# Sums of the last two expert groups kept per expert, and down weights loaded as neighbouring rows

## The chip, the cores and the metric

The kernel runs on one core of a Trainium2 chip. The metric is the device time of one execution in microseconds (us). It is compared by the median of several runs. One further execution was recorded by the hardware profiler; its span is counted from the first to the last instruction.

## The reference, cut to what matters

The layer normalises 256 tokens of width 1024, runs two kinds of attention, and adds the result to its input. Then comes a mixture of experts, which is where the change lies. There are 32 experts in four routing groups of eight; every token chooses one routing group and two experts in it.

```python
g = jnp.argmax(g_logits, axis=-1)
top_v, top_e = lax.top_k(e_logits, EXPERTS_PER_TOKEN)          # 2 per token
weight = p_group * jax.nn.softmax(top_v, axis=-1)
...
hid = jax.nn.silu(xc @ w_gate[e]) * (xc @ w_up[e])             # 1024 -> 256
return hid @ w_down[e]                                         # 256 -> 1024
...
y = jnp.zeros((N, D), t.dtype).at[slot_tok].add((out * slot_w[:, None]).astype(t.dtype))
```

Each expert owns three matrices of 1 MB in float32: gate, up and down. The order of the 256 hidden values does not matter, as long as the hidden vector and the rows of the down matrix have the same order.

## The kernel before, in words

**Weights.** Everything that is streamed from HBM is cut into 112 units of 1 MB (the list `units`, lines 77 to 102): 16 for the two projections, then for each expert its gate and up matrix, and its down matrix two experts later. They go into 23 slots of SBUF: a rotating pool `ring` of 16, and seven slots in other pools that become free later. `fill` (line 120) issues the load of the next unit when the unit that had its slot is done; all these loads stand in the queue of SyncE (SP), at line 138, and the very last unit is loaded in three pieces (line 141). A gate or up unit gives each partition 8 neighbouring rows of 1 KB (line 90); a down unit gives partition p the rows p and p + 128 of 4 KB each (line 92).

**One expert.** Each expert has up to 32 token slots. `gate` and `up` (lines 662 and 668) call `half`, 8 matrix products that put four partial sums into the four 32-partition strips of a PSUM bank, and copy the bank into SBUF, gate by ScalarE (ACT, line 665) and up by VectorE (DVE, line 670). `folded` (line 672) transposes these copies on TensorE (PE), four transposes, and DVE adds the partial sums (lines 678 and 680), which gives the hidden values. `down` (line 696) multiplies them with the down unit (line 693); the four column quarters of the result stand in four strips of one bank.

**Groups of four.** Four experts with neighbouring numbers form a group, eight groups in all (these are the kernel's groups, not the routing groups; group 6 is experts 24 to 27, group 7 is 28 to 31). `prep` (line 607) gathers the tokens of the next group: it needs the two 0/1 matrices `Ps` (lines 597 and 599), then 16 matrix products (line 615). For groups 0 to 6, `down` moves the result in four copies to a tile `oG` with 32 partitions for each expert (lines 707 and 709), `weighted` (line 633) multiplies the 0/1 matrix by the routing weights and transposes it once, and `combine` (line 723) adds the whole group to the sums `y` with 8 products of 128 rows (line 728). For group 7, `weighted_last` (line 620) makes four weighted matrices, one for each expert, all in the pass of expert 30, with the one pair of buffers `Ps`; the result of each expert stays in its strips (`moved`, line 711), and `spread` (line 715) adds one expert with 8 products of 32 rows, four strips side by side.

**Order of the work.** PE executes the products in the order in which the program lists them (`pe`, line 647). The main loop (lines 881 to 907) does for expert e: gate of e, fold of e - 1, at the third expert of a group the `combine` of the group before, up of e, at the fourth expert the `prep` of the next group, at the third expert `weighted`, then down of e - 2. The other engines' queues are ordered by the framework as operands become ready. At e = 28 there is `overflow` (line 755): every engine reads a flag and branches past a slow path, which the given data does not enter. After the loop come (lines 908 to 914) the spreads of experts 28 and 29, down of 30, the residual (`residual`, 8 products with the identity), the spread of 30, and `last`: down of 31 in two halves of columns, each followed by its own `moved`, `spread`, copies out of PSUM and two output transfers.

Of the kernel before, what the change touches and what calls it, by code (L numbers as in the profile page):

```python
# [9 lines left out]
F32 = mybir.dt.float32  # L10
# [4 lines left out]
AF = mybir.ActivationFunctionType  # L15
# [36 lines left out]
def hybrid_layer_kernel(ctx: ExitStack, tc: tile.TileContext, x, xt, w_in, w_out, w_gate, w_up, w_down, smalls, relb, out):  # L52
# [33 lines left out]
    def expert_unit(e, i):  # L86
        src = (w_gate, w_up, w_down)[i][e]
        place[e][i] = len(units)
        if i < 2:
            units.append((src.rearrange("(p k) f -> p k f", p=P), KC, 1))  # L90
        else:
            units.append((src.rearrange("(k p) f -> p k f", p=P), 2, 1))

    for e in range(E):
        expert_unit(e, 0)
# [491 lines left out]
    u = 16  # L587
    G = 4
    x2n = x2q.rearrange("t c k p -> t c p k")
    CROSS = [(j, c) for c in range(NC) for j in range(4)]  # L590
    g2p = A_COLS["g2p"][0]

    def places(g, c):
# [23 lines left out]
            gathered(st, q4, pg, 0, P)  # L617
        return st

    def weighted_last(st):  # L620
        t = pools["late"].tile([P, 2048], F32, name="oL", tag="late")
        st["o"], st["pT"] = t[:, :D].rearrange("p (i n) -> p i n", i=G), t[:, D:].rearrange("p (i t) -> p i t", i=G)
        for i in range(G):
            pt = ps.tile([P, 512], F32, name="ptr", tag="tr")
            for c in range(NC):
                q = st["P"][c][1].rearrange("p (j s) -> p j s", j=G)
                e = st["g"] * G + i
                nc.vector.tensor_scalar(q, st["P"][c][0][:, i : i + 1, :].broadcast_to([P, G, CAP]),
                                        W[:, c, e : e + 1], None, op0=ALU.mult)
                pe(nc.tensor.transpose(pt[:, c * P : (c + 1) * P], q.rearrange("p j s -> p (j s)"), ident))  # L630
            nc.scalar.activation(st["pT"][:, i, :], pt[:, :S], AF.Copy)

    def weighted(st):
        g = st["g"]
        if g == E // G - 1:
            return weighted_last(st)
        pt = ps.tile([P, 512], F32, name="ptr", tag="tr")
        for c in range(NC):
            q = st["P"][c][1].rearrange("p (g s) -> p g s", g=G)
            nc.vector.tensor_tensor(q, st["P"][c][0],  # L640
                                    W[:, c, g * G : (g + 1) * G].unsqueeze(2).broadcast_to([P, G, CAP]), op=ALU.mult)
            pe(nc.tensor.transpose(pt[:, c * P : (c + 1) * P], q.rearrange("p g s -> p (g s)"), ident))
        st["pT"] = ex.tile([P, S], F32, name="pT", tag="pT")
        st["o"] = ex.tile([P, D], F32, name="oG", tag="oG")
        nc.scalar.activation(st["pT"], pt[:, :S], AF.Copy)
# [4 lines left out]
    def half(e, st, i, low):  # L650
# [8 lines left out]
                                    start=r == 0, stop=r == KC // ROWS_Q - 1, tile_position=(0, q * CAP)))  # L659
        return t, pg  # L660

    def gate(e, st):
        t, pg = half(e, st, 0, place[e - 1][0] if e else None)
        st["parts"] = t
        nc.scalar.activation(t[:, :HID], pg[:, :HID], AF.Copy)
        return t

    def up(e, st, t):
        _, pg = half(e, st, 1, place[e][0])
        nc.vector.tensor_copy(t[:, HID : 2 * HID], pg[:, :HID])  # L670

    def folded(t):
        pt = ps.tile([P, 512], F32, name="ptr", tag="tr")
# [22 lines left out]
    def down(e, st, hT, low):  # L696
        i = e % G
        dv = unit(place[e][2], low).rearrange("p (c n) -> p c n", c=2)
        pd = ps.tile([P, 512], F32, name="pd", tag="tr")
        down_product(hT, dv, pd, range(2), range(4))  # L700
        if st["g"] == E // G - 1:
            moved(st, i, pd, slice(0, P))
            return
        for j in range(4):
            dst = st["o"][i * CAP : (i + 1) * CAP, j * 256 : (j + 1) * 256]
            if j % 2 == 0:
                nc.scalar.activation(dst, pd[j * 32 : (j + 1) * 32, :256], AF.Copy)  # L707
            else:
                nc.vector.tensor_copy(dst, pd[j * 32 : (j + 1) * 32, :256])  # L709

    def moved(st, i, pd, rows):
        nc.scalar.activation(st["o"][rows, i, :P], pd[rows, :P], AF.Copy)
        nc.vector.tensor_copy(st["o"][rows, i, P:], pd[rows, P:256])  # L713

    def spread(st, i, pairs):
        for j, c in pairs:
            r = slice(j * CAP, (j + 1) * CAP)
            pe(nc.tensor.matmul(y[j][:, c * 256 : c * 256 + 256], st["pT"][r, i, c * P : (c + 1) * P],  # L718
                                st["o"][r, i, :], start=False, stop=i == G - 1 and c == NC - 1, tile_position=(j * CAP, 0)))

    y = []

# [10 lines left out]
            pe(nc.tensor.matmul(y[j][:, c * 256 : c * 256 + 256], ident, res[:, c, j * 256 : (j + 1) * 256],  # L733
                                start=False, stop=False))

    def last(e, st, hT, res):
        dv = unit(place[e][2]).rearrange("p (c n) -> p c n", c=2)
        pd = ps.tile([P, 512], F32, name="pd", tag="tr")
        down_product(hT, dv, pd, (0,), range(4))
        warmed(2, "pp")  # L740
        for nh in range(2):
            down_product(hT, dv, pd, (1,), (2 * nh, 2 * nh + 1))
            moved(st, G - 1, pd, slice(nh * 64, nh * 64 + 64))
            j0 = 2 * nh
            spread(st, G - 1, [(j, c) for c in range(NC) for j in (j0, j0 + 1)])
            for c, eng in enumerate((nc.scalar, nc.sync)):
                for j in (j0, j0 + 1):
                    dst = res[:, c, j * 256 : (j + 1) * 256]
                    if j == j0:
                        nc.scalar.activation(dst, y[j][:, c * 256 : c * 256 + 256], AF.Copy)  # L750
                    else:
                        nc.vector.tensor_copy(dst, y[j][:, c * 256 : c * 256 + 256])  # L752
                eng.dma_start(out[c * P : (c + 1) * P, nh * 512 : nh * 512 + 512], res[:, c, nh * 512 : nh * 512 + 512])

    def overflow():
# [121 lines left out]
    with tc.issue_after(state["ps"].ins):  # L877
        nc.vector.tensor_reduce(cm, pc, axis=AX.X, op=ALU.max)
        nc.vector.tensor_copy(flag, cm)
    before, queue = None, []  # L880
    for e in range(1, E):
        g, i = divmod(e, G)
        old, old_t = st, t
        if i == 0:
            before, st = old, nxt
        t = gate(e, st)
        queue.append((e - 1, old, folded(old_t)))
        if i == 2 and g > 0:
            combine(before)
        up(e, st, t)  # L890
        if i == G - 1 and g < E // G - 1:
            nxt = prep(g + 1)
        if i == 2:
            weighted(st)
        if e == E - 1:
            hT = folded(t)
        if e > 1:
            down(*queue.pop(0), place[e][0])
        if e == OVER_E:
            overflow()  # L900
        if e == E - 1:
            rt_ = ring.tile([P, 2048], F32, name="res", tag="ring")
            res = rt_.rearrange("p (c n) -> p c n", c=NC)
            for c in range(NC):
                for nh in range(2):
                    nc.gpsimd.tensor_copy(res[:, c, nh * 512 : (nh + 1) * 512].rearrange("t (p k) -> t p k", k=KC),
                                          x2n[:, c, nh * 64 : (nh + 1) * 64, :])
    spread(st, 0, CROSS)
    spread(st, 1, CROSS)
    down(*queue.pop(0), place[E - 1][0])  # L910
    residual(0, res)
    residual(1, res)
    spread(st, 2, CROSS)
    last(E - 1, st, hT, res)


_OUTS = [((1, 256, 1024), "float32")]
# [71 lines left out]
```

## Time and profile before

| | |
|---|---|
| median of 3 runs | 344.23 us (343.37 to 344.47) |
| the profiled execution, its own time | 344.96 us |
| its span | 343.2 us |
| PE busy in the span | 314.5 us (92%) |
| DVE, ACT, POOL busy | 194.3, 139.9, 17.3 us |
| mean granted TensorE clock | 0.97 of full speed |
| read from HBM | 121.64 MB |
| SP queue, share of the 16 DMA engines | 89.1% |

The own time is 1.8 us above the span. A matrix product in float32 appears as two PE instructions, so "x16" is 8 products. The duration of a PE row is modelled and rows overlap; the distance between the starts of two rows that follow each other is what the first one costs. "[0.55 <-X]" at the end of a row is idle time of the engine before it and what ended it.

### The profile page before, as it was taken

The page shows a single profiled execution, that of the slowest core. Times are in us where ns is not written, and L with a number is a line of the kernel's source. Part 1 is how long each engine was busy: PE and PEld are TensorE (multiplying, and loading weights), DVE is VectorE, ACT ScalarE, POOL GpSimd, SP SyncE. Part 2 cuts the span into 40 slices and gives each one's busy share as a digit, 9 for nine tenths or more (in the row PEclk, how much of TensorE's full clock was granted, in tenths as well). Part 3 has the DMA queues.
Part 4 walks back from the last instruction along what each step waited for, and adds up shares of the span by engine and source line. Part 5 has one row for each costly group of instructions (what it writes and reads, how often), then busy time and mean ns, then how long its engine had stood idle before and what let it go on. Part 6 is the DMA issues. An engine that isn't in the chain of part 4 may idle for free. (4 is left out here: it accounts for less than half of the span.)

```text
span 343.2 us, 7327 instructions
## 1 busy us (share of the span) xinstructions
PE 314.5 (92%) x2801; PEld 217.4 (63%) x2801; DVE 194.3 (57%) x599; ACT 139.9 (41%) x364; POOL 17.3 (5%) x25
## 2 busy tenths in 40 slices
PE   6999999999999999999999999998489669968893
PEld 2758877788777797576666766566257326625461
DVE  1867858869998658665463654736224522532502
ACT  4876667968886443423232232321112211211302
POOL 1100001000110140000000000000000000040000
PEclk9899999999999999999999999999989978989997
DMA  6999999999635888899999999999999999999903
GB/s 197 403 385 317 389 387 402 413 411 409 209 99 210 319 355 320 303 423 418 416 416 415 415 421 418 413 421 413 416 418 416 418 415 420 416 411 420 362 10 122
DMA packets 29496, 123.20 MB, mean 359 GB/s; under 512 B 2295, under 2 KB 3364, under 8 KB 21268
## 3 DMA queue, kind: packets, MB, share of 16 engines
q1 hardware_dynamic: 28868, 121.17, 89.1%
q0 software_dynamic: 304, 1.02, 1.0%
q8 instruction: 23, 0.38, 0.4%
q10 hardware_dynamic: 288, 0.52, 0.4%
q14 instruction: 13, 0.11, 0.1%
HBM read 121.64 MB, written 1.07 MB: 358 GB/s over the span
## 5 line engine op out<-in xcount | busy, mean ns | idle before, releaser
L658 PE MATMUL pgu<-u,xe 128*32 128x256 f32 x976 | 67.4, 395 | 10.1 <-ACT oG L707 4.8
L254 PE MATMUL pp<-hi,xh 128*128 128x512 f32 (+1 forms) x132 | 53.3, 405 | 2.6 <-ACT hi L243 2.6
L254 PE MATMUL pp<-lo,xh 128*128 128x512 f32 (+1 forms) x132 | 52.1, 399 | 0.3 <-POOL lo L244 0.2
L254 PE MATMUL pp<-hi,xl 128*128 128x512 f32 (+1 forms) x132 | 51.9, 393 | 0.0
L707 ACT ACTIVATE oG<-pd 32x256 f32<-32x256 f32 x56 | 21.0, 374 | 75.0 <-PE pd L693 61.4
L658 PEld LDWEIGHTS pgu<-u,xe 128*32 128x32 f32 x976 | 29.5, 111 | 34.6 <-ACT oG L707 8.6
L244 DVE TENSOR_TENSOR lo<-u,hi 128x512 fp32r<-128x512 f32 x62 | 43.1, 714 | 13.0 <-ACT hi L243 12.7
L243 ACT ACTIVATE hi<-u 128x512 fp32r<-128x512 f32 x64 | 38.9, 626 | 18.3 <-PE pp L254 12.6
L709 DVE COPY oG<-pd 32x256 f32<-32x256 f32 x56 | 23.7, 423 | 38.7 <-ACT oG L707 36.8
L693 PE MATMUL pd<-u,hT 128*32 128x256 f32 x496 | 34.9, 394 | 6.6 <-DMA u<-in_w_down_dram 6.6
L254 PEld LDWEIGHTS pp<-hi,xh 128*128 128x128 f32 x132 | 25.1, 190 | 9.6 <-ACT hi L243 4.0
L254 PEld LDWEIGHTS pp<-lo,xh 128*128 128x128 f32 x132 | 25.3, 192 | 7.4 <-issue 1.0
L254 PEld LDWEIGHTS pp<-hi,xl 128*128 128x128 f32 x132 | 25.2, 191 | 4.6
L670 DVE COPY u<-pgu 128x256 f32<-128x256 f32 x30 | 12.7, 422 | 26.7 <-PE pgu L658 23.6
L615 PEld LDWEIGHTS pg<-Ps,x2q 128*128 128x128 f32 x224 | 25.5, 192 | 2.9 <-DVE gu L678 2.9
L693 PEld LDWEIGHTS pd<-u,hT 128*32 128x32 f32 x496 | 14.5, 112 | 20.0 <-DVE u L670 7.5
L615 PE MATMUL pg<-Ps,x2q 128*128 128x128 f32 x224 | 26.9, 278 | 0.0
L728 PE MATMUL y<-oG,pT 128*128 128x256 f32 x112 | 26.4, 391 | 0.0
L728 PEld LDWEIGHTS y<-oG,pT 128*128 128x128 f32 x112 | 21.8, 200 | 2.8
L678 DVE TENSOR_REDUCE gu<-ptr 128x64 f32<-128x256 f32 x32 | 13.6, 425 | 14.5 <-PE ptr L675 13.8
L675 PEld LDWEIGHTS ptr<-sm,u 128*128 128x128 f32 x120 | 13.4, 147 | 13.1 <-issue 9.9
L675 PE MATMUL ptr<-sm,u 128*128 128x128 f32 x120 | 21.0, 301 | 0.0
(166 smaller groups left out, 342.0 us busy)
## 6 DMA issues: line engine op xcount, KB each, us to landing
u<-in_w_up_dram SPq DMA_DIRECT2D x31, 1024.0 KB, 19.9
u<-in_w_gate_dram SPq DMA_DIRECT2D x30, 1024.0 KB, 19.9
u<-in_w_down_dram SPq DMA_DIRECT2D x30, 1024.0 KB, 19.9
u<-in_w_in_dram SPq DMA_DIRECT2D x11, 1024.0 KB, 12.0
u<-in_w_out_dram SPq DMA_DIRECT2D x4, 1024.0 KB, 14.6
x<-in_w_gate_dram SPq DMA_DIRECT2D x2, 1024.0 KB, 9.0
u<-in_w_in_dram SPq DMA_DIRECT2D x2, 512.0 KB, 6.0
x<-in_x_dram SPq DMA_DIRECT2D x2, 512.0 KB, 10.9
```

What stands on the lines that cost most here:

```text
L243: nc.scalar.activation(hi, raw, AF.Copy)
L244: (nc.gpsimd if u * 4 + k in (0,3,) else nc.vector).tensor_tensor(lo, raw, hi.bitcast(F32), op=ALU.subtract)
L254: yield lambda a=a, w=w, kk=kk, i=i: nc.tensor.matmul(pp, a, w[:, cols], start=first and kk == 0 and i == 0, stop=last and kk == len(hls) ...
L615: pe(nc.tensor.matmul(pg[:, j * P : (j + 1) * P], x2q[:, c, q4 * 4 + j, :], st["P"][c][1], start=c == 0, stop=c == NC - 1))
L658: pe(nc.tensor.matmul(pg[q * CAP : (q + 1) * CAP, :HID], st["xe"][:, k, j0 : j0 + CAP], wv[:, k, :], start=r == 0, stop=r == KC // ROWS_Q ...
L670: nc.vector.tensor_copy(t[:, HID : 2 * HID], pg[:, :HID])
L675: pe(nc.tensor.transpose(pt[:, j * P : (j + 1) * P], t[:, j * P : (j + 1) * P], ident))
L678: nc.vector.tensor_reduce(gu[:, :2], parts[:, :2], axis=AX.X, op=ALU.add)
L693: pe(nc.tensor.matmul(pd[j * 32 : (j + 1) * 32, :256], hT[:, c, :], dv[:, c, j * 256 : (j + 1) * 256], start=c == 0, stop=c == 1, tile_pos ...
L707: nc.scalar.activation(dst, pd[j * 32 : (j + 1) * 32, :256], AF.Copy)
L709: nc.vector.tensor_copy(dst, pd[j * 32 : (j + 1) * 32, :256])
L728: pe(nc.tensor.matmul(y[j][:, c * 256 : c * 256 + 256], st["pT"][:, c * P : (c + 1) * P], st["o"][:, j * 256 : (j + 1) * 256], start=st["g ...
```

## The change

The down unit gives partition p the rows 2p and 2p + 1, which lie side by side in HBM. To give the hidden values the same order, the copies of gate and up read every second element of the PSUM bank, first the even ones, then the odd ones (`paired`). Group 6 is treated like group 7: each expert keeps its own result and weighted matrix, and is added by `spread` one pass after its `down`; the `combine` of group 6 goes. The weighted matrices are made one per pass for group 6 and two per pass at experts 28 and 29 for group 7. Both groups' tiles, and the residual, take a slot of the `ring` pool. The first half of the residual is added in the pass of expert 30. `last` moves, spreads and writes the final expert once, not in two halves.

```diff
-            units.append((src.rearrange("(k p) f -> p k f", p=P), 2, 1))
+            units.append((src.rearrange("(p k) f -> p k f", k=2), 2, 1))
...
+    APART = E // G - 2
...
+    def spare(name):
+        used["ring"].append(len(units))
+        return ring.tile([P, 2048], F32, name=name, tag="ring")
...
+    def repeated(st, i):
+        e = st["g"] * G + i
+        for c in range(NC):
+            q = st["P"][c][1].rearrange("p (j s) -> p j s", j=G)
+            nc.vector.tensor_scalar(q, st["P"][c][0][:, i : i + 1, :].broadcast_to([P, G, CAP]),
+                                    W[:, c, e : e + 1], None, op0=ALU.mult)
+
+    def weighted_last(st, i):
+        pt = ps.tile([P, 512], F32, name="ptr", tag="tr")
+        for c in range(NC):
+            pe(nc.tensor.transpose(pt[:, c * P : (c + 1) * P], st["P"][c][1], ident))
+        nc.scalar.activation(st["pT"][:, i, :], pt[:, :S], AF.Copy)
...
+    def paired(dst, pg):
+        return dst.rearrange("s (c p) -> s c p", c=2), pg[:, :HID].rearrange("s (p c) -> s c p", c=2)
...
-        nc.scalar.activation(t[:, :HID], pg[:, :HID], AF.Copy)
+        nc.scalar.activation(*paired(t[:, :HID], pg), AF.Copy)
...
-        nc.vector.tensor_copy(t[:, HID : 2 * HID], pg[:, :HID])
+        nc.vector.tensor_copy(*paired(t[:, HID : 2 * HID], pg))
...
-        if st["g"] == E // G - 1:
-            moved(st, i, pd, slice(0, P))
+        if st["g"] >= APART:
+            moved(st, i, pd)
             return
...
+    def last(st, hT, dv, pd, res):
         for nh in range(2):
             down_product(hT, dv, pd, (1,), (2 * nh, 2 * nh + 1))
...
+        moved(st, G - 1, pd)
+        spread(st, G - 1)
+        for c in range(NC):
+            for j in range(4):
...
+            for nh, eng in enumerate((nc.scalar, nc.sync)):
                 eng.dma_start(out[c * P : (c + 1) * P, nh * 512 : nh * 512 + 512], res[:, c, nh * 512 : nh * 512 + 512])
...
+            if g >= APART:
+                last_group(st)
         t = gate(e, st)
         queue.append((e - 1, old, folded(old_t)))
-        if i == 2 and g > 0:
+        apart = () if g < APART else (i,) if g == APART else ((0, 1), (2, 3), (), ())[i]
+        if apart:
+            repeated(st, apart[0])
+        if i == 2 and 0 < g <= APART:
             combine(before)
         up(e, st, t)
+        for k, j in enumerate(apart):
+            if k:
+                repeated(st, j)
+            weighted_last(st, j)
         if i == G - 1 and g < E // G - 1:
             nxt = prep(g + 1)
-        if i == 2:
+        if i == 2 and g < APART:
             weighted(st)
+        if done:
+            spread(*done.pop())
...
         if e > 1:
-            down(*queue.pop(0), place[e][0])
+            e2, st2, hT2 = queue.pop(0)
+            down(e2, st2, hT2, place[e][0])
+            if st2["g"] >= APART:
+                done.append((st2, e2 % G))
         if e == OVER_E:
             overflow()
+            res = spare("res").rearrange("p (c n) -> p c n", c=NC)
...
+        if e == E - 2:
+            residual(0, res)
-    spread(st, 0, CROSS)
-    spread(st, 1, CROSS)
+    residual(1, res)
     down(*queue.pop(0), place[E - 1][0])
-    residual(0, res)
-    residual(1, res)
-    spread(st, 2, CROSS)
-    last(E - 1, st, hT, res)
+    spread(*done.pop())
+    dv = unit(place[E - 1][2]).rearrange("p (c n) -> p c n", c=2)
+    pd = ps.tile([P, 512], F32, name="pd", tag="tr")
+    down_product(hT, dv, pd, (0,), range(4))
+    spread(st, 2)
+    warmed(2, "pp")
+    last(st, hT, dv, pd, res)
```

## Rows read from the trace of the kernel before

**Rows 1.** Stretches; after the five engines: granted clock, DMA share, GB/s.

```profile
150.00:200.00 50.00, 50.00 (x633) 33.07 (x635) 27.48 (x79) 14.41 (x41) 0.00 (x0) 1.00 1.02 417
...
250.00:300.00 50.00, 43.67 (x448) 28.03 (x448) 19.41 (x54) 10.04 (x29) 0.00 (x0) 0.90 1.02 417
...
280.00:284.00 4.00, 3.45 (x25) 1.93 (x22) 1.02 (x3) 1.13 (x3) 0.00 (x0) 0.50 1.03 422
...
324.00:328.00 4.00, 4.00 (x66) 2.35 (x64) 1.28 (x4) 0.54 (x2) 0.00 (x0) 1.00 0.39 151
```

**Rows 2.** DMA packets of the span, and issues: count, size, us to landing.

```profile
DMA packets 29496, 123.20 MB, mean 359 GB/s; under 512 B 2295, under 2 KB 3364, under 8 KB 21268
...
u<-in_w_down_dram SPq DMA_DIRECT2D x20, 1024.0 KB, 20.0
```

**Rows 3.** Timeline of SP's queue: start of the issue, its duration, unit.

```profile
209.16 0.33 SPq L138 DMA_DIRECT2D u<-in_w_up_dram  x1
211.63 0.38 SPq L138 DMA_DIRECT2D u<-in_w_down_dram  x1
214.11 0.33 SPq L138 DMA_DIRECT2D u<-in_w_gate_dram  x1
216.68 0.33 SPq L138 DMA_DIRECT2D u<-in_w_up_dram  x1
219.14 0.38 SPq L138 DMA_DIRECT2D u<-in_w_down_dram  x1
221.63 0.33 SPq L138 DMA_DIRECT2D u<-in_w_gate_dram  x1
224.15 0.33 SPq L138 DMA_DIRECT2D u<-in_w_up_dram  x1
```

**Rows 4.** Timeline of PE, experts 26 to 29: start, duration, line, tile.

```profile
280.81 1.94 PE L658 MATMUL pgu<-u,xe 128*32 128x256 f32 x16 [0.55 <-ACT oG L707]
...
292.68 3.84 PE L615 MATMUL pg<-Ps,x2q 128*128 128x128 f32 x32
296.44 1.07 PE L693 MATMUL pd<-u,hT 128*32 128x256 f32 x16
297.33 1.05 PE L658 MATMUL pgu<-u,xe 128*32 128x256 f32 x16
298.31 0.66 PE L675 MATMUL ptr<-sm,u 128*128 128x128 f32 x4
298.90 1.07 PE L658 MATMUL pgu<-u,xe 128*32 128x256 f32 x16
...
304.42 1.07 PE L658 MATMUL pgu<-u,xe 128*32 128x256 f32 x16 [2.46 <-DVEq L758]
```

**Rows 5.** Timeline: `Ps` on DVE, `combine` of group 6, weighted transposes of group 7.

```profile
289.33 0.47 DVE L599 TENSOR_SCALAR Ps<-Pm,rstd 128x128 f32<-128x128 f32 x2
...
312.36 3.62 PE L728 MATMUL y<-oG,pT 128*128 128x256 f32 x16
...
316.91 0.44 PE L630 MATMUL ptr<-sm,Ps 128*128 128x128 f32 x2
...
317.72 0.52 PE L630 MATMUL ptr<-sm,Ps 128*128 128x128 f32 x2 [0.38 <-DVE Ps L628]
```

**Rows 6.** Timeline of the end: spreads, residual, last expert, last copies.

```profile
325.09 2.01 PE L718 MATMUL y<-oL 32*128 32x256 f32 x32
...
328.03 3.72 PE L733 MATMUL y<-res,sm 128*128 128x256 f32 x16
...
331.68 1.15 PE L718 MATMUL y<-oL 32*128 32x256 f32 x16
332.76 0.64 PE L693 MATMUL pd<-u,hT 128*32 128x256 f32 x8
...
335.18 1.13 PE L718 MATMUL y<-oL 32*128 32x256 f32 x8 [0.69 <-DVE oL L713]
...
338.94 0.76 DVE L752 COPY res<-y 128x256 f32<-128x256 f32 x2 [1.26 <-PE y L718]
```

## The prediction before the run

> **What bounds the kernel now.** I read the stretches first, then the queue that issues the weights, then TensorE (PE) in order of time. From 150 us on, the DMA engines are the bound: their share is 1.02 and they move 417 GB/s in the stretches 150 to 200 and 250 to 300 alike [rows 1]. SP's queue says the same in another way: it issues a unit of 1 MB every 2.5 us, and each lands 20 us after its issue [rows 2, 3], so eight are always under way and a new one starts as one ends. In that part PE's time is hidden: it idles 6.3 of the 50 us before 300.
>
> The end looks different. Between 324 and 328 us the rate falls to 151 GB/s, 0.6 MB in four microseconds [rows 1]: the last weights are in by about 327 us. Yet the last copy out of PSUM ends at 338.94 + 0.76 = 339.70 us, and from 325.09 on PE has work almost without a pause: two spreads, down of 30, the residual of 3.72 us, a spread, and then the last expert in two halves, each with its own move, spread and copies [rows 6]. So some 12 us after the weights are a chain of PE, and before it PE had gaps: at the third and fourth expert of a group it runs late because of `combine` (3.62 us) and `prep` (3.84 us), at the other two it waits for weights. Work that leaves the end and goes into those gaps is won. The thing to work out is how much PE can still take between 292 and 327 us.
>
> **The change part by part.** *Down weights.* A down unit consists of 256 packets of 4 KB, a gate or up unit of 128 of 8 KB; the page counts 29496 - 21268 = 8228 packets of 8 KB or more, about the 64 x 128 of gate and up, so rows that lie side by side do travel as one packet [rows 2]. The time of one unit is read from SP's queue: the issue that follows the end of unit n is that of unit n + 8, so the distance from a gate issue to the up issue behind it belongs to a down unit. These distances are 2.57 and 2.52 us, against 2.47, 2.48, 2.46 and 2.49 for the others [rows 3]. I take 0.07 us for each down unit; nothing and 0.10 are the ends. One comes every 7.5 us, so from 150 us to the landing of expert 26's gate at about 281 us there are 17: the weights are 1.2 us earlier there (0 to 1.7), and about 1.5 us earlier at the very end.
>
> *Copies of gate and up with stride two.* No row shows such a read out of PSUM. A copy of 128x256 out of PSUM takes 0.38 us [rows 6]; the ends are nothing and a doubling, 0.4 us more. I take nothing: the fold waits for these copies only a whole gate later (0.98 us [rows 4]); for the last expert a spread of 1.0 us stands between. Without that cover it would be 0.4 us once.
>
> *Slots.* Three tiles now sit in the ring. Worked through `fill`, the last unit then takes the slot of expert 25's gate, not that of 22's down, and that one is free once expert 25 is folded, five experts or some 37 us before the use; a landing takes 20 [rows 2], so the queue of eight is the nearer limit. Cost nothing. SP passes no new instruction before its last load; on POOL the four residual copies only move in the program, since nothing is queued ahead of them and they wait for DVE's branch at `overflow` either way; in the walk below the residual comes 10 us behind that branch.
>
> *PE, walked in program order.* Distances between starts give the prices [rows 4 to 6]: gate 298.31 - 297.33 = 0.98, fold 0.59, up like gate, together 2.55; down 0.89; `prep` 3.76; a spread 2.01 / 2 = 1.0; half the residual 3.65 / 2 = 1.83; the first weighted transpose 0.44, a second behind it 0.81, because DVE must rewrite `Ps` between them [rows 5]. The start is the gate of expert 26, which waited for its weights and then ran at half clock (1.94 us [rows 4], clock 0.50 [rows 1]). PE is late from there to `prep` at 292.68, so this moves with the weights: the up of 27 ends at 292.68 - 1.2 = 291.5.
> Expert 27: transpose 0.44, `prep` 3.76, spread 1.0, down 0.89. A new wait stands here: `Ps` of group 7 can only be written when group 6's last transposes have read it; before, they were written at 289.33, long ahead of `prep` [rows 5]. DVE writes a pair in 0.47 us; I take 0.5, ends 0 and 0.9 (with the copy of up ahead of it in DVE's queue). Behind it waits PE, nobody else. Sum 6.6, so 298.1 (before: 297.33).
> Expert 28: 2.55 + 0.44 + 0.81 + 1.0 + 0.89 = 5.7, so 303.8; then the branch at `overflow`, a hole of 2.46 us [rows 4], so 306.2 (before: 304.42).
> Expert 29: 5.7, so 311.9. Expert 30, without `combine`: 2.55 + 1.0 + 0.89 + 1.83 = 6.3, so 318.2. Expert 31: 2.55 + spread 1.0 + fold 0.59 + down 0.89 + residual 1.83 = 6.9, so 325.0.
> The end: down 0.89, spread 1.0, then first products, warming, second products and move as now (335.18 - 332.76 = 2.42), spread 1.08 between them, the last spread 1.13: 331.6. Four copies on each engine instead of two, 2 x 0.76 + 0.07: 333.1. That is 6.6 us before 339.70. The four output transfers now start within 1 us and not in two pairs 2 us apart; 1 MB at 417 GB/s is 2.5 us, of which about 0.4 cannot hide. **Sum: 6.6 - 0.4 = 6.2 us.** At the first products (326.9) the weights have been there for about 1.4 us, so no more than that could be added if PE were faster. The profiled execution took 344.96 us, so the sum makes 338.8; the median of the runs is 0.7 below it, so the forecast is 344.23 - 6.2 = 338.0.
>
> *A price that the rows dispute.* Each spread uses PE in strips of 32 rows between products of 128 rows, and the change puts seven of these switches into the loop. The spread at 331.68 stands between two such changes and costs 1.08 us, the two at 325.09, which share them, 1.0 each [rows 6]: a change of shape costs less than 0.1 us. The Trainium skill (TensorEngine Tiling (Array Packing), Key Properties) says that changing the tiling mode, not just the tile, drains TensorE. It gives no price; by it the time would be that of the third rival below, which is priced from rows.
>
> **The rivals.** *The packets bring nothing* (the down units stay at the common rate of 417 GB/s, so that the first part of the change does nothing): everything is 1.2 us later, 339.2. For it: the gap of 0.07 rests on six distances. Against: all of them agree.
> *DVE's waits are longer.* At experts 28 and 29 the second `Ps` may queue behind DVE's reductions and the copy of up; with the pair at 1.9 instead of 1.25 twice, 0.4 more at `prep`, and a wait of the same sort, 0.4, at each of experts 24, 25, 30 and 31, the gain shrinks by 3.3: 341.3. Against: at 317.72 the wait was 0.38 us.
> *PE drains.* If PE lets one shape end before the next begins, the overlap of two rows is lost at each switch. A down row lasts 1.07 us and the next one starts 0.89 after it [rows 4], so 0.18 at each of 14 switches, 2.5 us: 340.5. Against: the spread of 1.08 above, whose row of 1.15 still overlaps the next.
> *The clock falls; slower.* If PE, after the hole at `overflow`, runs experts 29 and 30 at half clock, as it ran after its waits before 281 us, each group of 16 instructions costs 0.87 more (1.94 against 1.07 [rows 4]); an expert has gate, up, down, spread and folds, so 3.9 us. It decides from about one and a half experts on; two make 7.8 - 6.2 = 1.6 us slower, 345.8. For it: the hole stays, and the gap at `prep` is new. Against: PE has little idle time between 298 and 318 us in the walk, and the mean clock over 250 to 300 was 0.90 even with the waits of before [rows 1].
>
> **How the numbers follow.** A measurement of this kernel tells about 0.3%, 1.0 us, from no change. Forecast (338.0, own range 336.2 to 339.0) 0.57; no gain from packets 0.13; longer waits 0.13; drain 0.05; clock 0.09; something else 0.03. Low end: the wait at `prep` nothing (0.5), the hole shorter since DVE moves two pieces and not four before its branch (0.8), packets at 0.10 (0.5): 336.2. High end: longer waits and no gain from packets together fall at 342.5; I stop at 342.0, which leaves out the clock, the rest and the worst sums of two, under 0.2. Faster: the first four, 0.88; same: a clock that takes just the 6 us (0.03) and most of the rest (0.02), 0.05; slower: the clock for longer (0.06) and a rest, 0.07.
>
> **What would show it.** In the profile after: `combine` 16 instructions fewer, spreads at each expert from 27 on with 1.0 us between starts; packets of 8 KB up by about 31 x 128; the distances in SP's queue equal; the last copy near 333 and PE's first products of the last expert a little behind its weights; granted clock 1.00 from 288 to 331. Wrong would be: the queue's distances unchanged, a gap before `prep` above 1 us, matmul groups of 1.9 us after 304 us, or spreads that cost clearly more than 1.08 each.

## The result, and the profile after

The changed kernel took 339.76 us (median of 4 runs, 339.21 to 340.34), the kernel before 343.8 beside it: a ratio of 0.9883, interval 0.9859 to 0.9906. That is 4.0 us; the sum had said 6.2. The profiled execution of the changed kernel took 340.34 us with a span of 338.6. The last copy out of PSUM ends 5.7 us earlier than before, the span 4.6 us.

The packets and the queue first, as in [rows 1, 2, 3]: the DMA page with the issue of down units, then SP's queue (start, duration, unit).

```profile
DMA packets 25528, 123.20 MB, mean 364 GB/s; under 512 B 2295, under 2 KB 3364, under 8 KB 13332
...
u<-in_w_down_dram SPq DMA_DIRECT2D x30, 1024.0 KB, 19.8
```

```profile
217.16 0.33 SPq L138 DMA_DIRECT2D u<-in_w_down_dram  x1
219.65 0.33 SPq L138 DMA_DIRECT2D u<-in_w_gate_dram  x1
222.16 0.33 SPq L138 DMA_DIRECT2D u<-in_w_up_dram  x1
```

Packets of 8 KB or more are now 25528 - 13332 = 12196, 3968 = 31 x 128 more, as forecast. The distance from gate to up, the one that belongs to a down unit, is 222.16 - 219.65 = 2.51 here against 2.57 and 2.52 in [rows 3].

Stretches (columns as in [rows 1]: granted clock, DMA share, GB/s at the end):

```profile
250.00:300.00 50.00, 44.70 (x466) 29.28 (x466) 20.11 (x62) 10.30 (x31) 0.00 (x0) 0.93 1.01 420
...
308.00:312.00 4.00, 4.00 (x38) 2.18 (x41) 0.00 (x0) 0.38 (x1) 0.00 (x0) 0.57 1.02 426
324.00:328.00 4.00, 4.00 (x48) 2.44 (x46) 0.69 (x3) 0.38 (x2) 0.00 (x0) 1.00 0.09 32
```

The rate in the bound part went from 417 to 420 GB/s, and between 324 and 328 us there is little left to load (32 instead of 151 GB/s): the weights end earlier. But for four microseconds behind the wait at expert 29 the mean granted clock is 0.57: PE ran most of them at the lower of its two levels.

PE from expert 26 on (start, duration, line, tile, the wait before it), which answers to [rows 4, 6]:

```profile
278.16 1.94 PE L664 MATMUL pgu<-u,xe 128*32 128x256 f32 x16 [1.32 <-DMA u<-in_w_gate_dram]
...
290.27 3.84 PE L615 MATMUL pg<-Ps,x2q 128*128 128x128 f32 x32 [0.37 <-DVE Ps L599]
294.04 1.15 PE L727 MATMUL y<-oL 32*128 32x256 f32 x16
295.11 1.07 PE L702 MATMUL pd<-u,hT 128*32 128x256 f32 x16
296.00 1.05 PE L664 MATMUL pgu<-u,xe 128*32 128x256 f32 x16
...
299.38 0.52 PE L638 MATMUL ptr<-sm,Ps 128*128 128x128 f32 x2 [0.37 <-DVE Ps L632]
...
303.34 1.07 PE L664 MATMUL pgu<-u,xe 128*32 128x256 f32 x16 [1.36 <-DVEq L763]
...
305.93 0.44 PE L638 MATMUL ptr<-sm,Ps 128*128 128x128 f32 x2
307.82 0.52 PE L638 MATMUL ptr<-sm,Ps 128*128 128x128 f32 x2 [1.46 <-DVE Ps L632]
308.28 1.89 PE L727 MATMUL y<-oL 32*128 32x256 f32 x16
310.10 1.93 PE L702 MATMUL pd<-u,hT 128*32 128x256 f32 x16
311.81 1.11 PE L664 MATMUL pgu<-u,xe 128*32 128x256 f32 x16
...
316.51 1.99 PE L742 MATMUL y<-res,sm 128*128 128x256 f32 x8
318.44 1.07 PE L664 MATMUL pgu<-x,xe 128*32 128x256 f32 x16
...
325.61 1.07 PE L702 MATMUL pd<-u,hT 128*32 128x256 f32 x16
326.61 1.15 PE L727 MATMUL y<-oL 32*128 32x256 f32 x16
```

Beside the walk:

| point | forecast | measured | distance, forecast | distance, measured |
|---|---|---|---|---|
| gate of 28 | 298.1 | 296.00 | | |
| gate of 29 | 306.2 | 303.34 | 8.1 | 7.3 |
| gate of 30 | 311.9 | 311.81 | 5.7 | 8.5 |
| gate of 31 | 318.2 | 318.44 | 6.3 | 6.6 |
| down of 30 | 325.0 | 325.61 | 6.8 | 7.2 |
| last copies end | 333.1 | 333.96 | 8.1 | 8.4 |

PE comes to expert 29 some 2.9 us ahead of the walk, loses 2.8 of it there, and another 0.9 between the gate of 30 and the last copies. What happens at expert 29 on the other engines is in the timeline of all engines:

```profile
303.53 4.16 POOL L923 COPY res<-x2q 128x512 f32<-128x512 f32 x4 [173.42 <-DMA u<-in_w_down_dram]
...
305.89 0.88 DVE L691 TENSOR_TENSOR hT<-gu 128x64 f32<-128x64 f32 x1
...
306.69 0.41 DVE L679 COPY u<-pgu 128x256 f32<-128x256 f32 x1
307.02 0.94 DVE L632 TENSOR_SCALAR Ps<-Pm,W 128x128 f32<-128x128 f32 x2
```

`hT` takes 0.88 us; over the last five experts its median is 225 ns. A pair of `Ps` takes 0.94, not 0.47 [rows 5]. Both run while POOL copies the residual. The copy out of PSUM between them has its usual length. The 0.65 us of `hT` and the 0.47 of the pair make up the 1.1 us by which the second transpose of expert 29 waits longer (1.46) than that of expert 28 (0.37); then the clock falls for the spread and the down.

In the kernel before, POOL's copies stand at the same place behind the branch; `hT` met only the end of one of them, and no `Ps` was due (timeline of all engines):

```profile
304.46 4.16 POOL L906 COPY res<-x2q 128x512 f32<-128x512 f32 x4 [174.22 <-DVEq L758]
...
307.40 0.29 DVE L682 TENSOR_TENSOR hT<-gu 128x64 f32<-128x64 f32 x1
```

The end (copies and output transfers):

```profile
332.55 1.41 DVE L756 COPY res<-y 128x256 f32<-128x256 f32 x4 [1.37 <-PE y L727]
333.42 0.86 ACTq L758 DMA_DIRECT2D out_dram<-res  x2
333.70 0.85 SPq L758 DMA_DIRECT2D out_dram<-res  x2
```

From the last copy, 332.55 + 1.41 = 333.96, to the end of the span are 4.64 us; before they were 343.2 - 339.70 = 3.5.

### The profile page after: what moved, and what is told of

It is laid out like the page before. It is cut to its first block, busy times and chain, and to the rows that moved or that the text cites. A ratio compares the mean times of both kernels' runs of the same rounds, so it can differ in the third digit from the quotient of the medians.

```text
span 338.6 us, 7426 instructions
## 1 busy us (share of the span) xinstructions
PE 314.3 (93%) x2855; PEld 216.6 (64%) x2855; DVE 193.7 (57%) x600; ACT 138.7 (41%) x362; POOL 17.7 (5%) x25
## 2 busy tenths in 40 slices
DMA packets 25528, 123.20 MB, mean 364 GB/s; under 512 B 2295, under 2 KB 3364, under 8 KB 13332
## 3 DMA queue, kind: packets, MB, share of 16 engines
HBM read 121.64 MB, written 1.07 MB: 362 GB/s over the span
## 5 line engine op out<-in xcount | busy, mean ns | idle before, releaser
L664 PE MATMUL pgu<-u,xe 128*32 128x256 f32 x976 | 66.6, 391 | 7.6 <-DMA u<-in_w_gate_dram 2.5
L716 ACT ACTIVATE oG<-pd 32x256 f32<-32x256 f32 x48 | 18.0, 375 | 57.9 <-PE pd L702 46.3
L718 DVE COPY oG<-pd 32x256 f32<-32x256 f32 x48 | 20.3, 423 | 28.9 <-ACT oG L716 27.2
L702 PE MATMUL pd<-u,hT 128*32 128x256 f32 x496 | 34.0, 391 | 2.6 <-DMA u<-in_w_down_dram 2.6
L737 PE MATMUL y<-oG,pT 128*128 128x256 f32 x96 | 23.4, 399 | 0.0
L737 PEld LDWEIGHTS y<-oG,pT 128*128 128x128 f32 x96 | 19.2, 206 | 2.6
```

Source lines behind the costliest of these rows:

```text
L664: pe(nc.tensor.matmul(pg[q * CAP : (q + 1) * CAP, :HID], st["xe"][:, k, j0 : j0 + CAP], wv[:, k, :], start=r == 0, stop=r == KC // ROWS_Q ...
L702: pe(nc.tensor.matmul(pd[j * 32 : (j + 1) * 32, :256], hT[:, c, :], dv[:, c, j * 256 : (j + 1) * 256], start=c == 0, stop=c == 1, tile_pos ...
```

## The experiments

**The two parts alone.** First the layout of the down weights and the strided copies on the kernel before, then the rest of the change without them. The first is this, with the strided copies that belong to it:

```diff
-            units.append((src.rearrange("(k p) f -> p k f", p=P), 2, 1))
+            units.append((src.rearrange("(p k) f -> p k f", k=2), 2, 1))
...
-        nc.scalar.activation(t[:, :HID], pg[:, :HID], AF.Copy)
+        nc.scalar.activation(*paired(t[:, :HID], pg), AF.Copy)
...
-        nc.vector.tensor_copy(t[:, HID : 2 * HID], pg[:, :HID])
+        nc.vector.tensor_copy(*paired(t[:, HID : 2 * HID], pg))
```

> Only the down weights and the copies of gate and up are as in the change; the last groups stay as before. Theory A (packets of 8 KB save some 0.07 us a unit, and the end follows the weights): SP's last weight issue 1.5 to 2.8 us earlier than 308.34 and the time 1.5 to 2.5 us shorter, 341.3 to 342.3. Rival B (the packets gain 0.02 to 0.03 us a unit, the jumps of 1.6 to 2 us in the issue times at 160 and 230 us are chance): last issue within 1 us of 308.34, time within 1 us of before. Rival C (the copies with stride two cost): their rows above 0.42 us and 0.38 us.

Measured: 342.98 us, ratio 0.9962 (0.9939 to 0.9984), so 1.3 us by the ratio, between what theory A and rival B expect. (The medians alone, 344.65 beside 342.98, would say 1.7; the gains below are by the ratio too.) SP's last weight issue in this profile, at 305.34, is 2.0 us earlier than in the repeat of before below. The hole at the branch stays as it was (PE's timeline):

```profile
301.48 1.52 PE L658 MATMUL pgu<-u,xe 128*32 128x256 f32 x16 [2.46 <-DVEq L761]
```

The second takes the same lines back in the changed kernel, the strided copies with them:

```diff
-            units.append((src.rearrange("(p k) f -> p k f", k=2), 2, 1))
+            units.append((src.rearrange("(k p) f -> p k f", p=P), 2, 1))
```

> The change without its packets: down weights and copies as before, last two groups expert by expert. Theory A: what is left of the 4.0 us is 1.5 to 2.5 us less, so 341.3 to 342.3, and the rows of the end are those of the changed kernel moved later. Rival B: the whole gain of about 4.0 us stays, 339.8. Under both, DVE's rows at expert 29 stay long (hT 0.88, Ps 0.94) if POOL's residual copies run beside them.

Measured: 340.76 us, 0.9915 (0.9882 to 0.9947), so 2.9 us, again between the two expectations. The two gains add up to 4.2, the change made 4.0: they are independent as far as these intervals tell, which is about 1 us. PE's timeline at expert 29:

```profile
309.07 0.52 PE L638 MATMUL ptr<-sm,Ps 128*128 128x128 f32 x2 [1.44 <-DVE Ps L632]
309.52 1.15 PE L724 MATMUL y<-oL 32*128 32x256 f32 x16
```

The wait is there too, so it belongs to the order of the work; the half clock is not. In SP's queue between 184 and 303 us the median distance of a down unit is 2.55, 2.53 and 2.54 us with packets of 4 KB (the kernel before, its repeat below, this run) and 2.50, 2.49 and 2.50 with 8 KB (the changed kernel, the first experiment, the repeat of the changed kernel), some 15 distances each; all other units have 2.47 to 2.50.

**The residual's copies on ACT.** If POOL's copies hold up DVE, ACT in their place should not.

```diff
-                    nc.gpsimd.tensor_copy(res[:, c, nh * 512 : (nh + 1) * 512].rearrange("t (p k) -> t p k", k=KC),
-                                          x2n[:, c, nh * 64 : (nh + 1) * 64, :])
+                    nc.scalar.activation(res[:, c, nh * 512 : (nh + 1) * 512].rearrange("t (p k) -> t p k", k=KC),
+                                         x2n[:, c, nh * 64 : (nh + 1) * 64, :], AF.Copy)
```

> The changed kernel with the four residual copies on ScalarE in place of GpSimd. Theory D (GpSimd's copies, 303.5 to 307.7 us, slow DVE's work on SBUF; PE waits 1.46 us for Ps at expert 29, then the clock falls and experts 29 and 30 lose 1.9 us more): hT back to 0.23, the pair of Ps to 0.47, the wait to 0.4, no half clock at 308 to 312, time 2.5 to 3 us below the changed kernel, about 337. Rival E (DVE is slow there because it comes out of the branch): the rows stay long, time as the changed kernel, 339.8. Rival F: the copies now delay ScalarE's own rows by about as much, 339 to 340.

Measured: 340.25 us, 0.988 (0.9844 to 0.9916). Timeline of all engines:

```profile
303.11 4.07 ACT L923 ACTIVATE res<-x2q 128x512 f32<-128x512 f32 x4 [1.00 <-DVEq L763]
...
307.63 0.23 DVE L691 TENSOR_TENSOR hT<-gu 128x64 f32<-128x64 f32 x1 [1.35 <-ACT gu L688]
307.77 0.48 DVE L632 TENSOR_SCALAR Ps<-Pm,W 128x128 f32<-128x128 f32 x2
308.11 0.53 PE L638 MATMUL ptr<-sm,Ps 128*128 128x128 f32 x2 [1.96 <-DVE Ps L632]
308.57 2.09 PE L727 MATMUL y<-oL 32*128 32x256 f32 x16
```

DVE's operations are back at 0.23 and 0.48 while no copy runs on POOL, at the same place behind the branch: the branch is not what made them long. But the copies of 4.07 us now stand in ACT's queue ahead of the activation that DVE needs for `hT`, and `Ps` stands behind `hT`. The wait only changed its owner, and the clock fell again. DVE's rows are those of theory D, the time that of the changed kernel, not the 337 that theory D had made of them.

**The last expert in two halves**, as in the kernel before, for the output transfers:

```diff
-        moved(st, G - 1, pd)
-        spread(st, G - 1)
+            moved(st, G - 1, pd, slice(nh * 64, nh * 64 + 64))
+            spread(st, G - 1, (2 * nh, 2 * nh + 1))
...
```

> The changed kernel, but the last expert is moved, spread, copied and sent in two halves of columns as before the change. Theory G (the single pass shortens PE's chain by about 1.1 us for a spread and 0.7 for a move, and gives back 0.76 us in copies and 1.1 us in the transfers that no longer overlap): time within 0.7 us of the changed kernel. Rival H (the single pass is the gain of the end): 2 us slower, 341.8. Rival I (it is a loss): over 0.7 us faster.

Measured: 341.35 us, 0.990 (0.9868 to 0.9933). Timeline of the end:

```profile
328.75 0.64 PE L702 MATMUL pd<-u,hT 128*32 128x256 f32 x8
...
336.01 0.76 DVE L756 COPY res<-y 128x256 f32<-128x256 f32 x2 [1.26 <-PE y L727]
```

The span is 340.2, so the tail after the last copy is 340.2 - 336.77 = 3.4 us, as in the kernel before, against 4.64. But the chain from the first products to the last copy is 8.0 us instead of 333.96 - 327.69 = 6.3. Together is better by some half a microsecond, as theory G has it, but that is less than the intervals tell. The wait for `Ps` at expert 29 is 1.47 us in this profile, and the spread and the down behind it run at half clock again: 3.2 us from 309.34 to 312.54.

**The residual's copies early**, ahead of expert 24, still on POOL; the slow path in `overflow` then adds to the copy.

```diff
+            if g == APART:
+                res = spare("res").rearrange("p (c n) -> p c n", c=NC)
...
+                        nc.gpsimd.tensor_copy(res[:, c, nh * 512 : (nh + 1) * 512].rearrange("t (p k) -> t p k", k=KC),
+                                              x2n[:, c, nh * 64 : (nh + 1) * 64, :])
...
-            overflow()
+            overflow(res)
```

> The changed kernel with the four residual copies on GpSimd moved ahead of the pass of expert 24 (the slow path, which is not entered, would add to the copy). There PE still waits for weights. Theory D (at expert 29 these copies slow DVE on GpSimd, or block ScalarE in the run before): hT 0.23 and a pair of Ps 0.47 at expert 29, PE waits 0.4 for Ps there and not 1.46, so 1 us less by the wait alone and up to 2.9 with a clock that stays at full speed; ratio 0.980 to 0.985. DVE's rows of experts 24 and 25 get longer in their place, without cost. Rival J (PE is held by something else in that pass): ratio as the changed kernel, 0.988.

Beside it the changed kernel again, without an edit:

> The changed kernel itself, once more, on the chip of the other three. Theory: ratio 0.986 to 0.991. In its profile the wait for Ps at expert 29 is again near 1.46 us (it comes from the order of the work); the half clock behind it may or may not come, as it did not in the run without the packets. If the wait is gone, it was chance.

Measured: early copies 338.63 us, 0.9846 (0.9821 to 0.9872); the repeat 339.92, 0.9887 (0.9862 to 0.9911). Timeline of the early copies:

```profile
307.02 0.47 DVE L632 TENSOR_SCALAR Ps<-Pm,W 128x128 f32<-128x128 f32 x2
...
307.35 0.52 PE L638 MATMUL ptr<-sm,Ps 128*128 128x128 f32 x2 [0.37 <-DVE Ps L632]
...
325.32 1.07 PE L702 MATMUL pd<-u,hT 128*32 128x256 f32 x16 [0.76 <-DMA u<-in_w_down_dram]
```

and of the repeat:

```profile
308.47 0.53 PE L638 MATMUL ptr<-sm,Ps 128*128 128x128 f32 x2 [1.45 <-DVE Ps L632]
308.93 1.15 PE L727 MATMUL y<-oL 32*128 32x256 f32 x16
...
310.89 1.05 PE L664 MATMUL pgu<-u,xe 128*32 128x256 f32 x16
```

With POOL quiet, the wait of 1.45 is back at 0.37, the value at expert 28, and 1.3 us of the time go with it by the medians; the two intervals still overlap by 0.001. What is late next are the weights: down of 30 waits for its own. The repeat has the wait and not the half clock, so the wait is regular and the clock a matter of the execution.

**Separate tiles for the weighted matrices**, so that DVE need not wait for PE to read `Ps`:

```diff
+            state["w"] = spare("Pw").rearrange("p (g i c s) -> p g i c s", g=2, i=G, c=NC)
...
-            q = st["P"][c][1].rearrange("p (j s) -> p j s", j=G)
+            q = st["w"][:, i, c, :].rearrange("p (j s) -> p j s", j=G)
...
-        if apart:
-            repeated(st, apart[0])
+        for j in apart:
+            repeated(st, j)
...
```

Both weighted matrices of a pass are now written ahead of its `up`.

> The changed kernel with a tile of its own for the weighted matrices of experts 24 to 31 in place of the one pair of buffers Ps, so that DVE never waits for PE's transposes. Theory: the gaps of 0.37 before the gather, 0.37 at expert 28 and 1.46 at expert 29 go from PE's rows, ratio 0.981 to 0.985. Rival K (GpSimd's copies still slow DVE at expert 29, so that the hidden values come late and another wait takes the place): the gap moves to the down of expert 27 or the fold, ratio 0.986 to 0.989.

Measured: 338.55 us, 0.9846 (0.9819 to 0.9873). PE's timeline:

```profile
308.74 1.07 PE L667 MATMUL pgu<-u,xe 128*32 128x256 f32 x16 [0.94 <-DMA u<-in_w_gate_dram]
...
311.23 1.07 PE L667 MATMUL pgu<-u,xe 128*32 128x256 f32 x16 [0.83 <-DMA u<-in_w_up_dram]
```

No wait for `Ps` is left behind the branch, though POOL's copies still hold `hT` up (0.88 us): no transpose is due behind it. PE gets to expert 30 ahead of its weights. The gain is that of the early copies, and here too PE then waits for weights.

**Both, and with fewer transfers or an earlier residual.** The first puts the two together and sends the output in two transfers of 512 KB, the second keeps four, the third also moves the residual's products one expert forward.

```diff
-            for nh, eng in enumerate((nc.scalar, nc.sync)):
-                eng.dma_start(out[c * P : (c + 1) * P, nh * 512 : nh * 512 + 512], res[:, c, nh * 512 : nh * 512 + 512])
+            (nc.sync, nc.scalar)[c].dma_start(out[c * P : (c + 1) * P, :], res[:, c, :])
```

> Both together (early residual copies, own tile for the weighted matrices), and two output transfers of 512 KB in place of four of 256 KB. Theory: PE's chain from expert 27 on has only the hole of the branch left; PE comes within about 1 us of the weights at the last expert; ratio 0.977 to 0.983. Rival L (the last weights are the bound as soon as 1 to 2 us are won): no better than the better one of the two alone. For the transfers: the time from the last copy out of PSUM to the end of the span 3.5 to 4 us instead of 4.6.

> Early residual copies and own tile for the weighted matrices, with the changed kernel's four output transfers. Theory (PE has caught up with the weights in either of the two alone, so the second adds nothing): ratio 0.983 to 0.987, PE waits for weights at experts 30 and 31. Rival O (the two transfers of 512 KB cost the 1 us by which the run with them was slower): ratio below 0.983 and 4.6 us, not 4.9, from the last copy to the end.

```diff
-        if e == E - 2:
-            residual(0, res)
-    residual(1, res)
+        if e >= E - 3 and e < E - 1:
+            residual(e - E + 3, res)
```

> As the run before it, and the two halves of the residual one pass earlier each, at experts 29 and 30, where PE waits for weights. Theory (what then bounds is the landing of the last two down units): PE's first products of expert 31's down move up by 0.5 to 1.9 us, ratio 0.979 to 0.985. Rival P (PE at expert 30 has less room than it seems, since gate and up wait 0.8 us each only): no change against the run before it.

Measured: 339.42 us, 0.9879 (0.9858 to 0.9901); 339.05, 0.9853 (0.9822 to 0.9884); 338.38, 0.9836 (0.9805 to 0.9867). Two transfers bring nothing: the tail in that profile is 4.9 us, against 4.6 with four in the second, and both forecasts of that run, 0.977 to 0.983 and 3.5 to 4 us, missed. The second came out as its theory says, the third inside its range. With the residual done earlier, nothing of PE's is left to do ahead of the down of 30, and PE waits for its weights (timeline of the third):

```profile
325.38 1.07 PE L705 MATMUL pd<-u,hT 128*32 128x256 f32 x16 [1.21 <-DMA u<-in_w_down_dram]
```

In the second run the same wait is 0.57 us. The 1.21 belongs to an execution with late weights: it took 340.10 us, above the median, and its last weights were issued at 308.00 us, against 305.59 in the second. The first products of the last down are not earlier in it (327.46 against 326.39), so the profiles do not bear out that forecast. What they do show is that PE waits for the last weights again.

**The kernel before again**, without an edit, for its profiled execution:

> The kernel before, unchanged, once more, for a second profile of it. Theory M (the profiled execution that the sum was made against had its weights late by more than 1 us from the stretch at 150 to 180 us, by chance, while the median execution had not): in this profile the last weight issue is 0.8 to 1.5 us earlier than 308.34, at 306.8 to 307.5, and the own time nearer to 343.8. Rival N (the weights of this kernel are always that late): last issue within 0.4 us of 308.34. Ratio 0.998 to 1.002 under both. The distances of down units stay 0.03 to 0.05 us above the others.

Measured: 344.57 us, 1.0006 (0.9985 to 1.0027); the profiled execution took 343.97, that of the forecast 344.96. SP's last issue of weights, at 308.34 in the forecast's execution, stands here at

```profile
307.35 1.95 SPq L141 DMA_DIRECT2D u<-in_w_down_dram  x1
```

The forecast's execution had its weights 1.0 us late beside this one.

**Residual copies in pieces.** The runs so far say that POOL's copies hold up DVE, not how.

```diff
-                for nh in range(2):
-                    nc.gpsimd.tensor_copy(res[:, c, nh * 512 : (nh + 1) * 512].rearrange("t (p k) -> t p k", k=KC),
-                                          x2n[:, c, nh * 64 : (nh + 1) * 64, :])
+                for nh in range(8):
+                    nc.gpsimd.tensor_copy(res[:, c, nh * 128 : (nh + 1) * 128].rearrange("t (p k) -> t p k", k=KC),
+                                          x2n[:, c, nh * 16 : (nh + 1) * 16, :])
```

> The changed kernel with the residual copied on POOL in 16 pieces of 128x128 instead of four of 128x512, at the same place behind the branch. The question is how POOL's copies hold up DVE at expert 29. Theory P, whole instructions: a DVE operation on SBUF that comes while a POOL copy runs starts only when that copy has ended. For it: in the changed kernel hT begins at 305.89 and ends at 306.77, and the third POOL copy runs from 305.61 to 306.69; in its second run hT ends at 307.42 and the copies, of 1.06 to 1.11 us from 304.18 on, pass from the third to the fourth at about 307.3. In the kernel before, where hT comes 0.2 us ahead of such a border, it takes only 0.29. With pieces of a quarter, some 0.27 to 0.35 us each, hT would take between 0.23 and 0.6 instead of 0.88, and the first of a pair of Ps no more than 0.6 instead of 0.74; the second transpose of expert 29 would wait 0.4 to 0.9 us instead of 1.45, and the time would be 338.9 to 339.7 against a kernel before of 344.2. Theory Q, shared bandwidth: while POOL copies, each DVE operation on SBUF takes about four times as long (hT) or twice as long (Ps); then pieces change nothing, hT takes 0.88 and a pair 0.94 as long as the copies last, the wait stays at 1.4 or more, and the time at 339.8 or above, since more instructions on POOL can only last longer.

The border between two copies in the changed kernel comes from the third one seen alone, in a narrow window of POOL's timeline:

```profile
305.61 1.08 POOL L923 COPY res<-x2q 128x512 f32<-128x512 f32 x1
```

Measured: 338.68 us, 0.9841 (0.9803 to 0.9879). Timeline of all engines, and one piece alone in a narrow window of POOL's:

```profile
303.91 5.62 POOL L923 COPY res<-x2q 128x128 f32<-128x128 f32 x16 [173.59 <-DMA u<-in_w_down_dram]
...
306.01 0.42 POOL L923 COPY res<-x2q 128x128 f32<-128x128 f32 x1
...
306.27 0.24 DVE L691 TENSOR_TENSOR hT<-gu 128x64 f32<-128x64 f32 x1
...
306.78 0.75 DVE L632 TENSOR_SCALAR Ps<-Pm,W 128x128 f32<-128x128 f32 x2
...
307.25 0.67 PE L638 MATMUL ptr<-sm,Ps 128*128 128x128 f32 x2 [0.51 <-DVE Ps L632]
```

POOL copies for longer in all (5.62 us instead of 4.16, a piece about 0.40), and `hT` and `Ps` lie in the midst of it; still `hT` takes 0.24 and the wait 0.51 instead of 1.46. Bandwidth shared in proportion would have left `hT` at 0.88 and the wait at 1.4 or more. The ends say more than the lengths: the piece from 306.01 ends at 306.43, and `hT` at 306.51. In all nine profiles with these copies behind the branch, of either kernel, `hT` ends 0.08 or 0.09 us after some copy of POOL's does, whether it took 0.24 us, 0.29 or 0.88. So DVE's operation finishes only behind the end of the copy that runs. The lengths lie in theory P's bounds; the time is a little below its 338.9 to 339.7.

## Why the prediction was right, and where its sizes were off

The direction and the range held, and so did the main mechanism: both parts gain. The down weights gave about what their step said; the other part, some 4.7 us of the sum (6.2 less 1.5), gave 2.9 alone. The forecast's 338.0 was 1.8 us short of 339.76.

- **Down weights: right.** Alone they gave 1.3 us, for 1.2 to 1.5. One unit costs some 0.04 to 0.05 us less, not 0.07; the rival that the packets bring nothing is out by the first experiment's interval, whose upper end is 0.9984. Copies with stride two cost nothing, as taken: 384 ns at the median on ACT and 424 on DVE, both as before.
- **The wait ahead of `prep`: right** in place, 0.37 for 0.5.
- **The hole at the branch: on the favourable side.** It is 1.36 us, not 2.46. The range's low end named the reason, that DVE moves two pieces and not four before its branch; the first experiment, where the pieces are as before, keeps 2.46. In both kernels PE goes on 0.7 us after DVE's last piece ends.
- **Expert 29, the step that failed:** "a second behind it 0.81, because DVE must rewrite `Ps` between them", together with "on POOL the four residual copies only move in the program". The second transpose came 307.82 - 305.93 = 1.9 us after the first. At expert 28 the step was right (299.38 - 298.57 = 0.81). At 29 POOL's copies, which I had costed at nothing since PE's residual comes later, ran beside `hT` and `Ps`. In the kernel before they ran at the same place behind the branch, but no `Ps` was due there. Moving them (0.9846 beside 0.9887 for the repeat) took the wait back to 0.37, cutting them to 0.51. This is the rival *DVE's waits are longer*, though not by its mechanism, and at one of its experts.
- **Luck behind the branch.** That the gate of 30 came at 311.81, for 311.9, is two errors that cancel. PE was 2.9 us ahead at expert 29: the gate of 26 began at 278.16, 2.65 us earlier than in [rows 4] and not 1.2; the `combine` behind it cost 284.63 - 280.93 = 3.7 us and not 287.86 - 283.59 = 4.3, with less of it at half clock; and the hole was shorter. Expert 29 then took 8.5 us instead of 5.7.
- **The clock, in part.** After that wait the spread and the down of 29 ran at half clock: 308.28 to 311.81 is 3.5 us, against 308.93 to 310.89, 2.0, in the repeat. The price is 1.6 us where it comes; the rival had priced two whole experts. It came in the profile of the change, with ACT's copies and with the last expert in halves, not in that of the repeat or of the second experiment.
- **The drain: not at the rival's price, but not for nothing.** A spread between products of 128 rows costs 295.11 - 294.04 = 1.07 us from start to start, as at [rows 6], where the walk has 1.0. A down costs 296.00 - 295.11 = 0.89 ahead of a gate, but 326.61 - 325.61 = 1.00 ahead of a spread, and as much ahead of the residual. The walk has six spreads at 1.0 and three such downs at 0.89, so I estimate 0.75 us for all of them, not nothing and not 2.5; "less than 0.1" for a change of shape was a little too low for the down. The Trainium skill (TensorEngine Tiling (Array Packing), Key Properties) has the rule that a change of the tiling mode drains TensorE; no row here tells whether that is what costs these 0.07 and 0.11 us.
- **The outputs: too small.** Of four transfers at once, "about 0.4" was to stay; the tail grew by 1.1 us. Halves give the old tail back, and lose more on PE than they win.
- **What the sum was set against.** The profiled execution of before had late weights and was 0.7 us above the median, as the text said; yet the whole sum was taken off the median. The repeat of before shows that lateness: its last weights are issued 1.0 us earlier, and its gate of 26 begins at 279.21, 1.6 us earlier than in [rows 4].

Profile against profile the sum fell short by 1.6 us: 344.96 - 340.34 = 4.6 for 6.2. The outputs are 0.7 of that. The other 0.9 is the last copies' 333.96 for 333.1, and it comes behind the gate of 30, mostly from the prices above and from half the residual at 318.44 - 316.51 = 1.93 instead of 1.83. Against the medians it is 1.8, because the profiled execution of before stood 0.7 above its median and that of the change 0.6.

In the repeat, whose clock did not fall, the last copies end at 331.57 + 1.42 = 332.99 against a walk to 333.1. There too PE is ahead at expert 29 (gate at 303.99 for 306.2), loses 1.2 in it by the wait and 0.9 behind it by the small prices.

The pieces alone (one edit, 338.68 us) or everything early (338.38) are faster than both kernels by their medians; their intervals still overlap those of the changed kernel a little. Which repair is best stays open: without the two transfers their ratios are 0.9836 to 0.9853, within each other's intervals, and where the copies or the tiles were moved, PE waits for weights in the profile.

## What to carry to other kernels

Copies put on an idle engine are not free because that engine is idle: look which engine's short operations run beside them, and whether PE waits for those; cut the copies into small instructions or run them where nobody is due. Make a sum against a profiled execution only after seeing how late its bound resource is, here the last issue of weights, beside a second execution. When work is moved out of the end, look at what the transfers at the end were hidden behind.

## What the hardware did that I had not expected

- **A DVE operation between SBUF tiles that meets a POOL copy finishes only behind that copy's end.** In the changed kernel the third copy ends at 305.61 + 1.08 = 306.69 and `hT`, which takes 0.23 alone, ends at 306.77; with pieces of 0.40 us it took 0.24. The distance from a copy's end to that of `hT` is 0.08 or 0.09 us in nine profiles of nine. The copy out of PSUM beside the same copies took 0.41, as ever. The Trainium skill (SBUF — State Buffer, Who interferes with whom) says that the port pair which VectorE and GpSimd share is an exclusive lock held for a whole instruction, not a division of bandwidth; by that rule, the trace agrees, with 0.08 us from the copy's end to that of `hT`.
- **The clock after a wait is not settled by the wait.** With waits of 1.36 and 1.46 us at the branch and at `Ps`, the granted clock in the four microseconds from 308 on was 0.57 in the profile of the change; with 1.36 and 1.45 in its repeat it stayed at 1.00. Among the other profiles with waits of about this length it fell once (1.36 and 1.47, the last expert in halves) and stayed once (1.36 and 1.44, the change without its packets). What decides is open.
- **Rows of 8 KB against 4 KB** are worth some 0.04 us in a 1 MB unit of 2.5, under 2%, on queues that are always full.
